# Eight experts of a mixture layer in another order: full and small ones in turn

## The chip, the cores and the metric

The kernel runs on one core of a Trainium2 chip. Its engines are TensorE (PE, matrix products), VectorE (DVE), ScalarE (ACT), GpSimd (POOL) and SyncE (SP, which here only issues the transfers of weights). The metric is the device time of one execution in microseconds (us); lower is better.

## The reference

Two decoder layers work on 256 tokens of width 1024. Each has a mixer (windowed attention beside a diagonal state-space part) and a feed-forward part. In the first layer the feed-forward part is dense; in the second each token goes to 2 of 8 experts, and it is this part that the change touches:

```python
def _swiglu(h, wg, wu, wd):
    return (jax.nn.silu(h @ wg) * (h @ wu)) @ wd

def _moe_swiglu(x2d, w_router, wg, wu, wd):
    logits = (x2d @ w_router).astype(jnp.float32)
    top_v, top_i = lax.top_k(logits, TOP_K)          # TOP_K = 2
    gates = jax.nn.softmax(top_v, axis=-1).astype(x2d.dtype)
    ...
    # every expert: its tokens' rows, SwiGLU with wg[e], wu[e] (1024 x 3584) and wd[e] (3584 x 1024),
    # times the gate, added to those tokens' rows
```

All is float32. The weights of the eight experts are 352 MB and are read once.

## The kernel before

**Tiles of weights.** An expert's inner width 3584 is cut into 7 chunks of 512. A chunk needs 12 tiles of weights of 128x1024 (512 KB each): 4 for the gate, 4 for the up product, 4 for the down product. So an expert has 84 tiles and the part has 672. Each tile is loaded by SP into a buffer `w` (`load`), copied by ACT into a rounded high part `wh`, and DVE subtracts to get the low part `wl` (`split`, line 524). The products are made of three fp32r products, high by high, low by high and high by low (`mm3`), so that they are nearly exact.

**Full and small experts.** After the routing the experts other than number 0 are sorted by how many tokens they got (`sort`). Four of them are full: 128 rows each, three matmuls of 512 columns for each half of a weight tile, 6 per tile (`glu_up`, `glu_down`). Four are small: at most 64 rows each, so that the high and the low part of the rows stand side by side in the 128 columns that PE holds, and 4 matmuls per tile do (`light_up`, `light_down`). The two halves of the result are then joined: ACT copies the lower 64 rows into `low`, and one more matmul adds them to the upper ones (`join`, line 1399), twice per chunk and twice when the expert is done. A tile costs DVE and ACT the same in both kinds. Tokens over these limits are handled by a part behind a branch (`overflow`) that is not entered here.

**Gathering and scattering rows.** `gather` builds a matrix of zeros and ones (`PP`) that picks an expert's tokens, multiplies the rows (`hnh`, `hnl`) with it on PE, and ACT and DVE write the scaled result as `xh` and `xl`. One gather serves expert 0, one expert 1, one experts 2 and 3 together; `gather_light` does the same for the four small ones at once (`PPl`, `lx`, `PTl`). A finished expert is scattered: `yh` by ACT, `yl` by DVE, matmuls by the transposed matrix, and DVE adds to the rows (`X`, `give`, line 1522).

**What sets the order.** The program is first recorded as a list of operations (`Plan.add`) and then ordered by a planner (`Plan.order`, line 234). It runs a clock per engine with a cost for each operation (`Plan.cost`, line 205) and picks on each engine the ready operation with the longest way to the end. Buffers of 128x1024 are 44 (`NM`), shared by `w`, `wh`, `wl`, rows and matrices; a load waits until one is free, and the buffers that it takes over are fixed by that plan. At most 5 `wh` are alive at a time from the fifteenth chunk on (`KR[7]`), 7 before (`LEAN`). Each engine then runs its instructions in that fixed order, held by semaphores alone. A load costs the planner its bytes at 360 GB/s.

**The order of experts.** `moe` (line 1438) goes through `j` from 0 to 7: four full ones, then four small ones. Rows of the next group are gathered near the end of the expert before it (`mark`). All recorded operations carry line 439, so that the names of tiles tell them apart. Below, a *turn* is one expert's 84 tiles.

Of the kernel before, what the change touches and what calls it, by code (L numbers as in the profile page):

```python
# [22 lines left out]
NE = 8  # L23
NCH = DFF // 512

HEAVY = 4
ROOM = 64
GROUPS = {0: (0,), 1: (1,), 2: (2, 3), 4: None}
HEADS = [0, 4, 1, 5, 2, 6, 3, 7]
EPS = 1e-6  # L30
BIG = 1e30
# [31 lines left out]
class Buf:  # L63
    def __init__(self, plan, kind, shape, dtype, name):
        self.kind, self.shape, self.dtype, self.name = kind, shape, dtype, name
        self.real = None
        self.log = []
        self.users = 0
        self.live = False
        self.cols = int(np.prod(shape[1:]))  # L70
# [72 lines left out]


class Plan:
    between = 0.0027

    def __init__(self):
        self.scratch = bacc.Bacc("TRN2", target_bir_lowering=False, num_devices=1)
        self.tensor, self.vector, self.scalar = Engine(self, "PE"), Engine(self, "DVE"), Engine(self, "ACT")  # L150
        self.gpsimd, self.sync = Engine(self, "POOL"), Engine(self, "DMA")
        self.ops = []
        self.after = []
        self.keep = self.floor = 0
        self.tag, self.bonus = None, {}
        self.most = self.turn = self.turns = 0
        self.n = 0
        self.named = {}
# [45 lines left out]
    @staticmethod  # L204
    def cost(eng, method, a, k):
        size = lambda v: int(np.prod(v.shape[1:]))
        if method == "registers":
            return 0.5
        if eng == "DMA":
            return int(np.prod(a[0].shape)) * 4 / 360e3 + 0.01  # L210
        n = max(size(v) for v in a if isinstance(v, View))
        if eng == "PE":
            if method == "transpose":
                return 2 * size(a[2]) / 2400 + 0.001
            if a[1].buf.dtype == F32R:
                return max(size(a[2]), 256) / 2400 + Plan.between
            return 4 * max(size(a[2]), size(a[1])) / 2400 + 0.0054
        if eng == "ACT":
            return 0.05 + n * 0.000876 + (0.06 if any(isinstance(v, View) for v in k.values()) else 0)
        if eng == "POOL":  # L220
            return max(0.35, 0.05 + n * 0.0006)
        if method in ("tensor_scalar", "tensor_copy"):
            fast = all(v.buf.kind != "ps" for v in a if isinstance(v, View))
            ptr = method == "tensor_scalar" and isinstance(a[2], View)
            return 0.066 + n * (0.00055 if fast else 0.00104) + 0.062 * ptr
        ptr = method in ("scalar_tensor_tensor", "tensor_scalar") and any(isinstance(v, View) for v in a[2:3])
        return 0.068 + n * 0.00104 + 0.062 * ptr
# [6 lines left out]
    def order(self, slots):  # L234
# [65 lines left out]
        while done < n:  # L300
# [83 lines left out]
            if e == "PE":  # L384
                if ticks.get(int(t / TICK) - 1, 0) < WARM:
                    cost *= 2
                m = int((t + cost) / TICK)
                ticks[m] = ticks.get(m, 0) + o["cols"]
# [53 lines left out]
class Kernel:  # L442
# [995 lines left out]
    def moe(self, R):  # L1438
        self.mg = gain = R["prm"][:, 90:98]
        self.plan.tag = "rs"  # L1440
        self.rs = rs = self.inv_rms(self.X, D, "fr")
        self.route(rs, gain)
        self.plan.tag = "moe"
        Plan.between = 0.0135
        self.hold = [self.slot.buf.log[-1][0]] if self.HOLD[0] else []
        self.spare = self.HOLD[1]
        mark, rest, hn = None, None, []
        e = self.a["moe"]
        for j in range(NE):
            if j in GROUPS:  # L1450
                first = j
                self.plan.after = [mark] if j else []
                PT, of, rse = self.gather(GROUPS[j], hn) if j < HEAVY else self.gather_light(hn)
                self.plan.after = []
            n = j - first
            acc = [self.bank(), self.bank()]
            for i in range(NCH):
                i == 0 and self.marks.append((f'e{j}', len(self.plan.ops) + 3))
                if i == self.gate_at - 1:
                    mark = len(self.plan.ops) + 1  # L1460
                if i == self.gate_at:
                    if j == 0:
                        hn = self.split_rows([mark])
                    mark = len(self.plan.ops) + 1
                if j:
                    w = [Late(lambda j=j, i=i, q=q: e[bass.ds(self.regs[j], 1), i, q].rearrange("o p n -> (o p) n")) for q in range(12)]
                else:
                    w = [e[0, i, q] for q in range(12)]
                self.ks = self.LEAN[1] if NCH * j + i < self.LEAN[0] else self.KR[7]
                if j < HEAVY:  # L1470
                    ht = self.glu_up(w[:8], lambda t, k: of(n, k), 1, rse[:, n:n + 1])
                    down, scatter, to = self.glu_down, self.scatter, [acc]
                else:
                    ht = self.light_up(w[:8], lambda k: of(n, k), rse[:, n:n + 1])
                    down, scatter, to = self.light_down, self.scatter_light, acc

                if rest:
                    rest[0](*rest[1:])
                rest = (down, i, w[8:], ht, to, scatter(j, n, PT, acc) if i == NCH - 1 else None)
        rest[0](*rest[1:])  # L1480
        return hn
# [12 lines left out]
    def scatter(self, place, j, PT, acc):  # L1494

        y = []

        def half(h):
            if not y:
                y.extend((self.M("yh", F32R), self.M("yl", F32R)))  # L1500
            c = slice(512 * h, 512 * h + 512)
            self.act(y[0][:, c], acc[h], AF.Copy)
            self.tt(y[1][:, c], acc[h], y[0][:, c].bitcast(F32), OP.subtract)
            self.give(place, h, [[(PT[:, t, j], y[i][:, c]) for i in range(2)] for t in range(2)])

        return half
# [15 lines left out]
    def give(self, place, h, ops):  # L1522
        c = slice(512 * h, 512 * h + 512)
        for t in range(2):
            bank = self.bank()
            for i in range(2):
                self.nc.tensor.matmul(bank, *ops[t][i], start=i == 0, stop=i == 1)
            x = self.X[t][:, c]
            self.stt(x, bank, self.sgt[:, 8 * t + place:8 * t + place + 1], x, OP.mult, OP.add)
            if place == NE - 1:  # L1530
                self.nc.sync.dma_start(self.a["out"][t][:, c], x)

    def overflow(self, hn):
# [199 lines left out]
```

## Time and profile before

| | |
|---|---|
| median of 3 runs | 1472.16 us (1465.4 to 1474.07) |
| profiled execution | 1471.39 us |
| its span, first to last instruction | 1469.5 us |
| PE, DVE, ACT busy | 95%, 84%, 71% of the span |
| TensorE clock granted, mean | 0.988 |
| read from memory | 420 MB |

The page gives busy time of each engine over the whole span. The part with the eight experts fills the stretch from about 490 to 1465 us; the mixers and the dense part come before it. PE's busy time is drawn from modelled ends of pipelined matmuls: PE shows busy while matmuls follow each other, and its share says little of stretches in which it waits between them.

### The profile page before, as it was taken

To read this page: it belongs to the slowest core of one execution; us is meant where nothing else is said; L and a number is where in the kernel's file an instruction comes from. 1 tells how busy PE (TensorE), PEld (TensorE's weight loads), DVE (VectorE), ACT (ScalarE), POOL (GpSimd) and SP (SyncE) were. 2 spreads that over 40 slices of the span, in tenths; PEclk is the share of its full clock that TensorE was granted. 3 is DMA by queue.
4 is the path that set the end of the run, shared out by engine and by line. 5 is a ranking of instruction groups with operands and counts; after the bars stand their busy time and mean duration, and the time that the engine had idled before them with its cause. 6 is when DMAs were issued, how large, how long until landed. Compare 5 with 4: busy or idle time off the path is not lost. (4 is left out here: it accounts for less than half of the span.)

```text
span 1469.5 us, 20817 instructions
## 1 busy us (share of the span) xinstructions
PE 1400.5 (95%) x6558; PEld 1065.1 (72%) x6558; DVE 1239.3 (84%) x1668; ACT 1047.4 (71%) x1350; POOL 25.5 (2%) x44
## 2 busy tenths in 40 slices
PE   7999999999999999999999999998988899899897
PEld 4888888888888888888888888885666565555553
DVE  7888984454785899888889999989998999998987
ACT  5586754444455578777678777878787888888885
POOL 3000100000000000000000000000000000000000
PEclk9999999999999899999999999999999999999998
DMA  5356255555358499899899999989999999999993
GB/s 213 111 175 219 72 177 184 189 183 169 106 196 295 156 341 333 298 355 372 321 370 357 350 377 349 363 320 374 356 365 353 338 378 378 380 382 356 370 385 135
DMA packets 116901, 422.59 MB, mean 288 GB/s; under 512 B 13360, under 2 KB 13872, under 8 KB 116784
## 3 DMA queue, kind: packets, MB, share of 16 engines
q1 hardware_dynamic: 116784, 421.20, 77.8%
q8 instruction: 53, 0.87, 0.2%
q14 instruction: 64, 0.52, 0.1%
HBM read 420.10 MB, written 1.05 MB: 287 GB/s over the span
## 5 line engine op out<-in xcount | busy, mean ns | idle before, releaser
L439 DVE TENSOR_TENSOR wl<-w,wh 128x1024 fp32r<-128x1024 f32 x786 | 918.6, 1217 | 101.3 <-ACT wh L439 65.8
L439 ACT ACTIVATE wh<-w 128x1024 fp32r<-128x1024 f32 x786 | 783.7, 1052 | 113.2 <-PE bank L439 54.4
L439 PE MATMUL bank<-wl,lx 128*128 128x512 f32 x448 | 190.5, 428 | 22.2 <-DVE wl L439 21.9
L439 PE MATMUL bank<-wh,lx 128*128 128x512 f32 x448 | 176.2, 402 | 12.5 <-ACT sg L439 9.2
L439 PE MATMUL bank<-wh,xh 128*128 128x512 f32 x448 | 173.7, 393 | 1.1 <-ACT wh L439 0.6
L439 PE MATMUL bank<-wh,xl 128*128 128x512 f32 x448 | 171.9, 392 | 0.0
L439 PE MATMUL bank<-wl,xh 128*128 128x512 f32 x448 | 170.2, 393 | 0.8 <-DVE wl L439 0.8
L439 PEld LDWEIGHTS bank<-wl,lx 128*128 128x128 f32 x448 | 85.2, 190 | 84.3 <-DVE wl L439 65.7
L439 PE MATMUL bank<-wh,hth 128*128 128x512 f32 x336 | 114.2, 397 | 0.0
L439 PE MATMUL bank<-wl,hth 128*128 128x512 f32 x336 | 113.2, 396 | 0.0
L439 PE MATMUL bank<-wh,htl 128*128 128x512 f32 x336 | 112.8, 396 | 0.0
L439 PEld LDWEIGHTS bank<-wh,lx 128*128 128x128 f32 x448 | 85.5, 191 | 29.3 <-ACT sg L439 12.9
L439 PE MATMUL bank<-wl,ht 128*128 128x512 f32 x224 | 93.1, 434 | 9.6 <-DVE wl L439 9.3
L439 PEld LDWEIGHTS bank<-wl,xh 128*128 128x128 f32 x448 | 84.1, 188 | 20.8 <-DVE wl L439 3.5
L439 PEld LDWEIGHTS bank<-wh,xh 128*128 128x128 f32 x448 | 83.7, 188 | 18.4 <-ACT wh L439 1.4
L439 PEld LDWEIGHTS bank<-wh,xl 128*128 128x128 f32 x448 | 83.7, 188 | 17.7 <-DVE xl L439 0.3
L439 PE MATMUL bank<-wh,hh 128*128 128x512 f32 (+1 forms) x288 | 91.5, 385 | 0.4
L439 PE MATMUL bank<-wl,hh 128*128 128x512 f32 (+1 forms) x288 | 90.1, 381 | 0.0
L439 PE MATMUL bank<-wh,hl 128*128 128x512 f32 (+1 forms) x288 | 89.9, 380 | 0.0
L439 PE MATMUL bank<-wh,ht 128*128 128x512 f32 x224 | 85.8, 414 | 0.6 <-ACT wh L439 0.3
L439 ACT ACTIVATE low<-bank 64x512 fp32r<-64x512 f32 x64 | 37.9, 594 | 56.2 <-PE bank L439 55.8
L439 PEld LDWEIGHTS bank<-wh,htl 128*128 128x128 f32 x336 | 62.6, 188 | 13.0 <-DVE wl L439 0.2
(306 smaller groups left out, 1695.6 us busy)
## 6 DMA issues: line engine op xcount, KB each, us to landing
w<-in_moe_dram SPq DMA_DIRECT2D x672, 512.0 KB, 5.7
w<-in_dense_dram SPq DMA_DIRECT2D x84, 512.0 KB, 4.2
w<-in_wo_dram SPq DMA_DIRECT2D x16, 512.0 KB, 4.0
w<-in_win_u_dram SPq DMA_DIRECT2D x8, 512.0 KB, 5.7
w<-in_win_q_dram SPq DMA_DIRECT2D x8, 512.0 KB, 7.8
w<-in_win_kv_dram SPq DMA_DIRECT2D x4, 512.0 KB, 3.6
w<-in_wglu_dram SPq DMA_DIRECT2D x4, 512.0 KB, 3.6
X<-in_x_dram SPq DMA_DIRECT2D x2, 512.0 KB, 4.1
```

The costliest lines, as they stand in the source:

```text
L439: getattr(engines[o["eng"]], o["method"])(*map(real, o["a"]), **{n: real(v) for n, v in o["k"].items()})
```

## The change

The experts are taken in the order 0, 4, 1, 5, 2, 6, 3, 7: a full one, a small one, and so on. The rows of all four small experts are therefore gathered near the end of the first turn; those of expert 1 in the second turn, those of 2 and 3 in the fourth. Their results are kept by expert (`rows`). The planner's cost of a load falls too: 390 GB/s in place of 360 in the part with the experts. The last expert is number 7, as before.

```diff
-GROUPS = {0: (0,), 1: (1,), 2: (2, 3), 4: None}
+LIGHT = tuple(range(HEAVY, NE))
+
+TURNS = (0, 4, 1, 5, 2, 6, 3, 7)
+GROUPS = {0: (0,), 1: (1,), 2: (2, 3), 4: LIGHT}
...
-            return int(np.prod(a[0].shape)) * 4 / 360e3 + 0.01
+            return int(np.prod(a[0].shape)) * 4 / Plan.rate + 0.01
...
-        Plan.between = 0.0135
+        Plan.between, Plan.rate = 0.0135, 390e3
...
-        for j in range(NE):
+        rows = {}
+        for turn, j in enumerate(TURNS):
             if j in GROUPS:
-                first = j
                 self.plan.after = [mark] if j else []
-                PT, of, rse = self.gather(GROUPS[j], hn) if j < HEAVY else self.gather_light(hn)
+                got = self.gather(GROUPS[j], hn) if j < HEAVY else self.gather_light(hn)
                 self.plan.after = []
-            n = j - first
+                for n, i in enumerate(GROUPS[j]):
+                    rows[i] = (n, *got)
+            n, PT, of, rse = rows[j]
...
-                self.ks = self.LEAN[1] if NCH * j + i < self.LEAN[0] else self.KR[7]
+                self.ks = self.LEAN[1] if NCH * turn + i < self.LEAN[0] else self.KR[7]
...
-            if place == NE - 1:
+            if place == TURNS[-1]:
```

What comes before the experts keeps its order on every engine. In it, three places moved that matter below. First, DVE before, near the end of the second full expert, where the rows of experts 2 and 3 are gathered (`PP` is the picking matrix, `xl` the low part of the rows):

```order
L439 TENSOR_TENSOR wl<-w,wh 128x1024
L439 TENSOR_SCALAR PP<-K,sslot 128x128 x4
L439 TENSOR_TENSOR wl<-w,wh 128x1024
L439 COPY rse<-bank 128x2
L439 TENSOR_TENSOR wl<-w,wh 128x1024 x2
L439 SCALAR_TENSOR_TENSOR xl<-bank,prm_1063,xh 128x256 x2
L439 TENSOR_TENSOR wl<-w,wh 128x1024 x2
L439 SCALAR_TENSOR_TENSOR xl<-bank,prm_1063,xh 128x256 x2
L439 TENSOR_TENSOR wl<-w,wh 128x1024 x2
L439 SCALAR_TENSOR_TENSOR xl<-bank,prm_1063,xh 128x256 x2
L439 TENSOR_TENSOR wl<-w,wh 128x1024 x2
L439 SCALAR_TENSOR_TENSOR xl<-bank,prm_1063,xh 128x256 x2
```

The same engine now, in the second full expert's turn (the third turn):

```order
L443 TENSOR_TENSOR wl<-w,wh 128x1024 x10
L443 SCALAR_TENSOR_TENSOR sg<-bank,rse,sg 128x512
L443 TENSOR_TENSOR wl<-w,wh 128x1024 x3
L443 TENSOR_TENSOR htl<-bank,hth 128x512
L443 TENSOR_TENSOR wl<-w,wh 128x1024 x9
L443 SCALAR_TENSOR_TENSOR sg<-bank,rse,sg 128x512
```

Only the splits of weights and the expert's own steps are left there. The gather stands in the small expert's turn that follows (the fourth):

```order
L443 SCALAR_TENSOR_TENSOR sg<-bank,rsl,sg 64x512
L443 TENSOR_TENSOR wl<-w,wh 128x1024 x2
L443 TENSOR_SCALAR PP<-K,sslot 128x128 x4
L443 TENSOR_TENSOR wl<-w,wh 128x1024
L443 TENSOR_TENSOR ht_8817<-bank,ht_8817 128x4x64
L443 SCALAR_TENSOR_TENSOR sg<-bank,rsl,sg 64x512
L443 SCALAR_TENSOR_TENSOR xl<-bank,prm_1063,xh 128x256 x2
L443 TENSOR_TENSOR wl<-w,wh 128x1024
L443 SCALAR_TENSOR_TENSOR xl<-bank,prm_1063,xh 128x256 x6
L443 COPY rse<-bank 128x2
L443 TENSOR_TENSOR wl<-w,wh 128x1024 x12
```

So a gather that stood among a full expert's tiles now stands among a small one's; that of the single expert 1 likewise went from the first turn to the second. Last, ACT in a later small expert before, one whole chunk (`low` is a join, `ht` the input of the down product):

```order
L439 ACTIVATE wh<-w 128x1024 x3
L439 ACTIVATE low<-bank 64x512
L439 ACTIVATE wh<-w 128x1024 x2
L439 ACTIVATE ht_11743<-bank 128x4x64
L439 ACTIVATE wh<-w 128x1024 x6
L439 ACTIVATE low<-bank 64x512
L439 ACTIVATE wh<-w 128x1024
L439 ACTIVATE sg<-bank,rsl 64x512
```

and now, in the second small expert's turn:

```order
L443 ACTIVATE wh<-w 128x1024 x7
L443 ACTIVATE low<-bank 64x512
L443 ACTIVATE wh<-w 128x1024 x5
L443 ACTIVATE low<-bank 64x512
L443 ACTIVATE sg<-bank,rsl 64x512
L443 ACTIVATE ht_8540<-bank 128x4x64
L443 ACTIVATE wh<-w 128x1024 x4
L443 ACTIVATE ht_8602<-bank 128x4x64
L443 ACTIVATE wh<-w 128x1024 x3
L443 ACTIVATE low<-bank 64x512
L443 ACTIVATE wh<-w 128x1024 x3
L443 ACTIVATE low<-bank 64x512
L443 ACTIVATE wh<-w 128x1024 x8
```

The steady pattern that the third and fourth small turn had before, where a `low` comes two splits after the last tile that it needs, is gone: now 3 to 12 splits lie between, and the distance changes from chunk to chunk, as it did before in the first two small turns (2 to 7 there).

## Rows read from the trace of the kernel before

**Rows 1.** The page: span and busy time of each engine, its share, instructions.

```profile
span 1469.5 us, 20817 instructions
...
PE 1400.5 (95%) x6558; PEld 1065.1 (72%) x6558; DVE 1239.3 (84%) x1668; ACT 1047.4 (71%) x1350; POOL 25.5 (2%) x44
```

**Rows 2.** Windows, one per turn from the second: length, busy time (instructions), clock, DMA share, rate.

```profile
core 0: us, PE busy (x) PEld busy (x) DVE busy (x) ACT busy (x) POOL busy (x), PEclk, DMA share, GB/s
614.00:738.50 124.50, 124.50 (x584) 103.36 (x584) 111.31 (x113) 94.48 (x108) 0.00 (x0) 1.00 0.96 355
738.50:857.10 118.60, 118.60 (x536) 96.90 (x535) 108.02 (x104) 93.58 (x102) 0.00 (x0) 1.00 0.97 360
857.10:981.50 124.40, 124.40 (x587) 102.80 (x586) 112.80 (x119) 95.22 (x109) 0.00 (x0) 1.00 0.93 345
981.50:1096.00 114.50, 101.43 (x413) 72.47 (x411) 110.50 (x112) 96.69 (x115) 0.00 (x0) 0.97 0.96 366
1096.00:1217.30 121.30, 106.31 (x413) 72.80 (x414) 113.14 (x114) 99.01 (x118) 0.00 (x0) 0.96 0.95 361
1217.30:1335.70 118.40, 107.67 (x388) 61.60 (x388) 107.69 (x105) 99.61 (x118) 0.00 (x0) 1.00 0.99 379
1335.70:1455.00 119.30, 108.50 (x392) 62.33 (x392) 108.59 (x105) 99.64 (x117) 0.00 (x0) 1.00 0.88 332
```

**Rows 3.** Windows: the splits on DVE (`wl`) in full and small turns.

```profile
614.00:981.50 367.50, 183.84 (x507) 94.54 (x507) 293.72 (x253) 1.00 0.95 354
981.50:1455.00 473.50, 280.41 (x677) 128.72 (x678) 390.24 (x337) 0.98 0.94 360
```

**Rows 4.** Waits of DVE and ACT, first small turn (981.5 to 1096): total us, times, longest.

```profile
DVE wl L439 <- ACT wh L439: 3.3, 4, 1.8
...
ACT low L439 <- PE bank L439: 11.3, 7, 6.2
```

**Rows 5.** The same of the third small turn (1217.3 to 1335.7).

```profile
DVE wl L439 <- ACT wh L439: 6.8, 12, 0.7
DVE sg L439 <- PE bank L439: 3.2, 6, 0.5
...
ACT low L439 <- PE bank L439: 13.4, 14, 2.1
```

**Rows 6.** Gather of expert 1: duration ns min/median/max, first and last start.

```profile
L439 PE MATMUL bank<-PP,hnh x16: 221/274/275, 590.3 to 593.6; 128*128 128x128 f32 x16
L439 DVE TENSOR_SCALAR PP<-K,sslot x2: 279/280/280, 589.7 to 589.9; 128x128 fp32r<-128x128 f32 x2
...
L439 DVE SCALAR_TENSOR_TENSOR xl<-bank,prm,xh x8: 339/343/353, 594.2 to 596.8; 128x128 fp32r<-128x128 f32 x8
```

**Rows 7.** Gather of experts 2 and 3, DVE.

```profile
L439 DVE TENSOR_SCALAR PP<-K,sslot x4: 280/282/284, 712.0 to 712.6; 128x128 fp32r<-128x128 f32 x4
...
L439 DVE SCALAR_TENSOR_TENSOR xl<-bank,prm,xh x8: 476/478/484, 717.1 to 727.9; 128x256 fp32r<-128x256 f32 x8
```

**Rows 8.** Scatter's low part on DVE: all, and by line in the second pure window (738.5 to 857.1).

```profile
L439 DVE TENSOR_TENSOR yl<-bank,yh x16: 669/676/686, 758.0 to 1460.3; 128x512 fp32r<-128x512 f32 x8, 64x512 fp32r<-64x512 f32 x8
...
L439 DVE TENSOR_TENSOR yl<-bank,yh 128x512 fp32r<-128x512 f32 x4 | 2.7, 685 | 0.0
```

**Rows 9.** Who waited for a load of weights, full turns, then small ones.

```profile
ACT wh L439 <- DMA w<-in_moe_dram: 2.3, 4, 1.2
...
DVE wl L439 <- DMA w<-in_moe_dram: 0.4, 1, 0.4
```

**Rows 10.** The DMA queue's own waits for buffers, full turns, then small ones.

```profile
SPq L439 <- PE bank L439: 203.3, 164, 4.2
...
SPq L439 <- PE bank L439: 233.6, 252, 3.4
```

**Rows 11.** DMA issues: count, KB each, median us from issue to landing.

```profile
w<-in_moe_dram SPq DMA_DIRECT2D x672, 512.0 KB, 5.7
```

**Rows 12.** A window in which the clock fell, early in the second small turn.

```profile
1112.60:1119.40 6.80, 6.17 (x15) 4.82 (x16) 6.80 (x10) 5.53 (x6) 0.00 (x0) 0.50 0.69 264
```

More of the change, by code (lines that the diff above doesn't have):

```diff
@@ L145 @@
 class Plan:
-    between = 0.0027
+    between, rate = 0.0027, 360e3
     def __init__(self):
+        Plan.between, Plan.rate = 0.0027, 360e3
         self.scratch = bacc.Bacc("TRN2", target_bir_lowering=False, num_devices=1)
@@ L1468, in moe @@
                     w = [e[0, i, q] for q in range(12)]
-                self.ks = self.LEAN[1] if NCH * j + i < self.LEAN[0] else self.KR[7]
+                self.ks = self.LEAN[1] if NCH * turn + i < self.LEAN[0] else self.KR[7]
                 if j < HEAVY:
-                    ht = self.glu_up(w[:8], lambda t, k: of(n, k), 1, rse[:, n:n + 1])
+                    ht = self.glu_up(w[:8], lambda t, k, n=n, of=of: of(n, k), 1, rse[:, n:n + 1])
                     down, scatter, to = self.glu_down, self.scatter, [acc]
                 else:
-                    ht = self.light_up(w[:8], lambda k: of(n, k), rse[:, n:n + 1])
+                    ht = self.light_up(w[:8], lambda k, n=n, of=of: of(n, k), rse[:, n:n + 1])
                     down, scatter, to = self.light_down, self.scatter_light, acc
```

## The prediction

> **What bounds the kernel now.** I began with the page's busy shares [rows 1]: PE 95%, DVE 84%, ACT 71%, so no engine is full over the whole span and the question is which one is full where. The windows, one per turn of 84 tiles, answer it [rows 2] (the first turn, left out, is treated below). The count of splits shows that the cuts are right: 253 and 337 for three and four turns, against 252 and 336 [rows 3]. In the full turns PE is busy in every microsecond (118.60 of 118.60) while DVE has 10.6 us to spare. A full turn is thus a matter of PE's work alone. In the small turns the reader is to see the opposite: PE has gaps, and DVE is busy for 110.50 of 114.50, then 113.14 of 121.30, 107.69 of 118.40 and 108.59 of 119.30 us. So a small turn is DVE's work plus what DVE idles: 4.0, 8.2, 10.7 and 10.7 us. The waits say where the idling comes from [rows 4, 5]. ACT, which runs in a fixed order, sits at `low` until PE has finished a bank (11.3 and 13.4 us); the `wh` queued behind it come late, and DVE waits for those (3.3 and 6.8 us). The weights themselves are not late: 2.3 us were waited for loads in the full turns and 0.4 in the small ones [rows 9], while the DMA queue waited over 200 us in either half for a buffer to come free [rows 10]. Yet it isn't far from its end: busy 0.93 to 0.99 of the time except in the last turn, which runs out of loads [rows 2].
>
> **Which time the sum is made against.** The profiled execution took 1471.39 us, 1.9 more than its span and 0.8 below the median of 1472.16.
>
> **Full turns: gathers leave them.** The third turn, with no gather, took 118.60 us; the second, with that of experts 2 and 3, took 124.50, and the fourth, with that of the small ones, 124.40 [rows 2]. A gather on PE's path costs 5.9 and 5.8 us. After the change the order leaves the second to fourth full expert with their own work: minus 11.7. The first turn gets the small experts' gather for that of expert 1. The latter's matmuls take 3.3 us from first to last start [rows 6], which is interleaved, so about 3.6; the other I price at its 5.8 of a full turn: plus 2.2, between nothing (both are 32 matmuls) and 5.8. Sum: **minus 9.5**.
>
> **Small turns: DVE gets more to do.** Added to DVE's 439.9 us in the four windows: for expert 1, 2 x 0.280 + 8 x 0.343 = 3.3 us [rows 6]; for experts 2 and 3, 4 x 0.282 + 8 x 0.478 = 5.0 [rows 7]; and 4 `yl` at 0.68 that stood in a full turn [rows 8] and stand in a small one now, 2.7. ACT's share of these (xh, yh) lies beside, since ACT has 18 to 22 us free per small turn [rows 2]. PE's share costs nothing there as long as PE has gaps. That makes 450.9 us of work. The scatters of the full experts were in small turns already, and those of the small experts stay in them.
>
> **Small turns: what DVE idles.** This can't be read from the trace, since the order of ACT and DVE is new. Bounds: 4.0 us per turn, as the first small turn had, which is the only one that follows a full turn, as all will; and 10.7, as the third and fourth had. Its `low` is early by no fixed distance, as in the first two turns of before. I take 6.0, the middle of the first two (4.0 and 8.2), so 24 us in all. Four small turns then take 474.9 us instead of the present 473.5: **plus 1.4**. With 4.0 it would be minus 6.6, with 10.7 plus 20.2.
>
> **The cheaper load in the planner** costs no instruction. It changes the order, which is in the term above, and how early buffers are handed to loads. **Held tiles:** 44 buffers carry the rows too. Before, a full turn held 8 at most (4 of all rows, 4 of experts 2 and 3) and a small one 9; now both kinds stand together and up to 13 are held. Some 4 loads less are ahead, of 512 KB [rows 11]. At 118.6 / 84 = 1.4 us per tile that is 6 us of cover. I cost it at nothing, because nobody waits for loads now [rows 9]; if the cover goes, that is the third rival.
>
> **Sum:** 1471.4 - 9.5 + 1.4 = **1463 us**, 0.6% below the median. Its own range is 1455 (idle 4.0) to 1472 (idle 8.2).
>
> **What a page says of such a change.** The Trainium skill, Perfetto Trace Analysis, Optimization Strategy, says that a kernel whose most contended engine changes over time may gain by interleaving those regimes. The rows show the two regimes, PE full in one half and DVE in the other. By that rule alone a pair of turns would approach the larger of DVE's and PE's work. DVE's is 108 + 112.7 = 221 us per pair where I have 118.6 + 118.7 = 237, which would be 4 x 16 = 64 us less. The trace does not bear that out at this grain: at most 5 `wh` tiles are split ahead, and 5 tiles are 7 us of a turn of 118. Only the seams can overlap. I give it 0.02.
>
> **Rival 1, faster: seams and idling both gain.** At each of the three new seams from full to small, DVE may run 5 tiles ahead of PE at 98 / 84 = 1.16 us (390.24 / 337 [rows 3]) instead of 1.41: 3 x 5 x 0.25 = 4 us. And if more splits ahead of `low` free DVE to idle 2 us per turn, 16 us go. That gives 1463 - 20 = **1443**. For it speaks the first small turn, where a full turn's lead was used up; against it that even there `low` waited 11.3 us [rows 4]. Chance 0.27.
>
> **Rival 2: no better order.** The small turns idle as the third and fourth do, 10.7 us each: 1463 + 18.8 = **1482**, within 1%. For it: the second small turn had an irregular order too and lost 8.2, with a lower clock (0.96) [rows 2]; a piece of it ran at 0.50, the lower of the two levels, 1.2 GHz [rows 12]. Against: it is the worst of four. Chance 0.12.
>
> **Rival 3, slower: the stream of weights becomes the bound.** My sum asks for 84 tiles, 44.0 MB, in 118.7 us, which is 371 GB/s in every turn. The full turns saw 345 to 360 [rows 2]. If buffers come free later because 13 are held, and the rate stays at 360, each of seven turns takes 122.3 us: 856 instead of 355.8 + 474.9 = 830.7, so **1489**. It decides as soon as the lead is used up, and `wh` would then wait for loads. For it: the DMA share is 0.93 to 0.99. Against: 379 GB/s were reached in the third small turn, and the lower rates stand where the queue waited for buffers [rows 10]. Chance 0.13.
>
> The Trainium skill, DMA: Bandwidth & Descriptors, Where 436 GB/s comes from, sets the memory side at about 358 GB/s per core; by that figure a turn would be 123.0 us, an estimate, and the sum 1494. The 379 of the third small turn [rows 2] are above it, so here the measurement decides against it as a ceiling.
>
> **Chances and range.** A run of this kernel tells about 1% from no change, so the marks are 1457.4 and 1486.9. Forecast 0.45, of which 0.08 lies below 1457; rivals 0.27, 0.12, 0.13; full interleaving 0.02; 0.01 for what I have not thought of. Faster: 0.27 + 0.08 + 0.02 = 0.37; same: 0.37 + 0.12 = 0.49; slower: 0.13 + 0.01 = 0.14. From 1440 to 1486 the range leaves out some 0.08 below and 0.12 above.
>
> **What would show it.** In the profile after: the third, fifth and seventh turn at 117 to 119 us with PE busy throughout; if they stay near 124, the first term is wrong. Small turns of 114 to 122 us with DVE busy 110 to 116 and idle 4 to 8; the fourth turn longest, since the larger gather is in it. Waits of `wh` for loads still in single microseconds; tens would mean rival 3. A clock of 0.50 in stretches that begin full turns, where PE is the bound, would cost half their length and would break the sum.

## The result and the profile after

The changed kernel takes **1454.3 us** (median of 4 runs, 1451.65 to 1456.36); before, in the same comparison, 1470.71. The ratio is 0.9891, interval 0.9854 to 0.9928: 1.1% faster, just past the mark of 1457.4 that told faster from the same, though the interval (0.7 to 1.5%) takes in that mark of 1%. 1463 was forecast: the time lies 0.7 us below the forecast's own range of 1455 to 1472, and inside the whole range of 1440 to 1486. The profiled execution took 1456.36 us, 15.0 less than the one of before [rows 1].

The page's first lines hardly differ from those of before: less idle time, the same work.

```profile
span 1454.5 us, 20913 instructions
...
PE 1395.2 (96%) x6558; PEld 1085.9 (75%) x6558; DVE 1239.1 (85%) x1668; ACT 1049.5 (72%) x1350; POOL 25.4 (2%) x44
```

The windows, one per turn, tell more. The first line is the first turn; then small and full turns alternate, beginning with a small one (columns as in [rows 2]).

```profile
core 0: us, PE busy (x) PEld busy (x) DVE busy (x) ACT busy (x) POOL busy (x), PEclk, DMA share, GB/s
465.20:615.60 150.40, 147.59 (x703) 118.89 (x702) 131.69 (x220) 104.44 (x125) 0.00 (x0) 0.98 0.72 260
...
615.60:736.90 121.30, 112.00 (x450) 80.08 (x449) 111.28 (x118) 101.42 (x125) 0.00 (x0) 0.93 0.95 361
736.90:853.30 116.40, 116.40 (x528) 96.09 (x527) 106.48 (x100) 89.97 (x99) 0.00 (x0) 1.00 1.00 385
853.30:975.90 122.60, 111.61 (x453) 79.39 (x452) 116.34 (x125) 103.47 (x127) 0.00 (x0) 0.94 0.96 369
975.90:1091.70 115.80, 115.80 (x525) 95.57 (x524) 107.62 (x101) 92.72 (x100) 0.00 (x0) 1.00 0.99 375
1091.70:1206.60 114.90, 104.02 (x408) 74.19 (x407) 110.95 (x110) 100.48 (x117) 0.00 (x0) 0.94 0.99 377
1206.60:1321.90 115.30, 115.30 (x523) 93.84 (x522) 105.52 (x100) 91.40 (x102) 0.00 (x0) 1.00 1.00 386
1321.90:1439.30 117.40, 109.11 (x413) 74.49 (x412) 112.81 (x113) 99.78 (x118) 0.00 (x0) 0.94 0.82 315
```

The reader is to see two things. The full turns take 115 to 116 us with PE busy throughout; of those before only the one without a gather, 118.60, comes near [rows 2]. The small turns take 115 to 123, with DVE busy for all but 10.0, 6.3, 4.0 and 4.6 us.

| term | before | forecast | measured |
|---|---|---|---|
| first turn | 148.7 | +2.2 | +1.7 (150.4) |
| second to fourth full expert | 367.5 | 355.8 | 347.5 |
| small turns | 473.5 | 474.9 | 476.2 |
| of that DVE's work | 439.9 | 450.9 | 451.4 |
| of that DVE's idle time | 33.6 | 24.0 | 24.8 |

The differences, 1.7 - 20.0 + 2.7 = -15.6, make up the span's -15.0; what is missing stands before the first turn and after the last.

The first turn of before, which had no row yet:

```profile
465.30:614.00 148.70, 145.97 (x694) 120.77 (x693) 129.66 (x214) 103.29 (x125) 0.00 (x0) 0.97 0.77 279
```

From 615.6 us on, loads are waited for as little as before [rows 9], and ACT sits at `low` for 17.8 us in four small turns, where one turn took 11.3 or 13.4 [rows 4, 5]. First the wait for loads, then that of `low` (total, times, longest):

```profile
DVE wl L443 <- DMA w<-in_moe_dram: 0.4, 1, 0.4
...
ACT low L443 <- PE bank L443: 17.8, 22, 1.8
```

### The profile page after: what moved, and what is told of

It is laid out like the page before. It is cut to its first block, busy times and chain, and to the rows that moved or that the text cites. A ratio compares the mean times of both kernels' runs of the same rounds, so it can differ in the third digit from the quotient of the medians.

```text
span 1454.5 us, 20913 instructions
## 1 busy us (share of the span) xinstructions
PE 1395.2 (96%) x6558; PEld 1085.9 (75%) x6558; DVE 1239.1 (85%) x1668; ACT 1049.5 (72%) x1350; POOL 25.4 (2%) x44
## 5 line engine op out<-in xcount | busy, mean ns | idle before, releaser
L443 PE MATMUL bank<-wh,lx 128*128 128x512 f32 x448 | 181.6, 413 | 18.6 <-ACT sg L443 15.1
L443 PE MATMUL bank<-wl,lx 128*128 128x512 f32 x448 | 186.3, 418 | 5.6 <-DVE wl L443 5.3
L443 PE MATMUL bank<-wl,hth 128*128 128x512 f32 x336 | 115.8, 397 | 0.0
L443 PE MATMUL bank<-wh,hth 128*128 128x512 f32 x336 | 115.7, 398 | 0.0
L443 PE MATMUL bank<-wl,ht 128*128 128x512 f32 x224 | 84.5, 420 | 1.7 <-DVE wl L443 1.7
L443 PEld LDWEIGHTS bank<-wh,hth 128*128 128x128 f32 x336 | 62.3, 188 | 13.9 <-issue 0.5
```

Of the source, the lines that this page charges most:

```text
L443: getattr(engines[o["eng"]], o["method"])(*map(real, o["a"]), **{n: real(v) for n, v in o["k"].items()})
```

## Experiments

Each was timed against the kernel before. The column "2 to 7" is, in the profiled execution, the stretch from the first `wh` of the second turn to the first of the eighth; "8" goes from there to the end of the last `wh`. They leave out what happens before the experts, which a different order also shifts. Medians come from four comparisons, in which the kernel before took 1468.7 to 1472.3, so that kernels are better compared by their ratios. With the cost only and at 375 GB/s the traced execution was the fastest of its kernel's, 8.3 and 5.1 us below the median.

| kernel | median us | ratio, interval | 2 to 7 | 8 |
|---|---|---|---|---|
| before | | 1 | 721.7 | 118.7 |
| the change | 1454.3 | 0.9891 (0.9854 to 0.9928) | 706.3 | 113.6 |
| cost only | 1474.82 | 1.0033 (1.0019 to 1.0047) | 712.5 | 115.3 |
| turns only | 1473.69 | 1.0029 (1.0014 to 1.0043) | 722.2 | 118.2 |
| gather in a full turn | 1460.16 | 0.9934 (0.9914 to 0.9954) | 709.5 | 115.3 |
| less PE in full turns | 1441.38 | 0.9810 (0.9791 to 0.9828) | 686.2 | 120.4 |
| less DVE in small turns | 1447.28 | 0.9854 (0.9833 to 0.9876) | 698.4 | 113.7 |
| chunks alternate | 1455.23 | 0.9898 (0.9869 to 0.9927) | 706.1 | 112.7 |
| gaps filled | 1456.33 | 0.9917 (0.9898 to 0.9937) | 706.0 | 113.3 |
| cheap from the fifth turn | 1458.50 | 0.9930 (0.9908 to 0.9951) | 707.1 | 122.9 |
| cost only, gaps filled | 1469.15 | 0.9976 (0.9963 to 0.9989) | 716.0 | 114.6 |
| 375 GB/s | 1464.74 | 0.9958 (0.9941 to 0.9975) | 707.7 | 121.6 |
| 420 GB/s | 1461.66 | 0.9922 (0.9897 to 0.9946) | 709.0 | 110.9 |
| 40 buffers | 1473.90 | 0.9999 (0.9984 to 1.0014) | 704.5 | 116.2 |

**Each half of the change alone.** The old order of experts with the cheaper load:

```diff
-        Plan.between = 0.0135
+        Plan.between, Plan.rate = 0.0135, 390e3
```

> The old order of experts, and only the planner's load at 390 GB/s. If the gain came from work that leaves the full turns (theory: a full turn is PE's work), those stay at 124.5, 118.6 and 124.4 us, and only the small turns change, by DVE's idle time: 0 to -8 us in all, 1463 to 1471. If the gain came from the cheaper load (rival), the time is near 1455.

The new order with the old cost:

```diff
-        Plan.between, Plan.rate = 0.0135, 390e3
+        Plan.between, Plan.rate = 0.0135, 360e3
```

> The new order of experts with the planner's load at 360 GB/s. By the theory the full turns stay at 115 to 117 us and the small turns may idle more, up to 10.7 us each: 1455 to 1472. By the rival (the cheaper load did it) the time goes back to about 1470, with the full turns long again.

Neither is faster: 1.0033 and 1.0029, both intervals above 1, and both together 0.9891. The new order at 360 GB/s starts well (its third turn, full, takes 115.7 us), but its fifth and sixth turn are these:

```profile
970.90:1095.50 124.60, 123.18 (x536) 95.66 (x534) 110.83 (x108) 91.21 (x103) 0.00 (x0) 1.00 0.98 359
1095.50:1213.70 118.20, 107.29 (x397) 64.67 (x397) 107.82 (x106) 98.18 (x115) 0.00 (x0) 1.00 0.99 374
```

The seventh and eighth repeat them (124.9, 118.2). In the small one DVE idles 10.4 us, about the 10.7 of the two last turns of before. In the full one PE looks busy, yet it is fed piece by piece, as the waits of its fifth turn show (total, times, longest; PEld is the load of a block of weights into PE):

```profile
PEld bank L443 <- DVE wl L443: 4.9, 10, 0.7
...
SPq L443 <- DVE wl L443: 45.6, 53, 2.6
...
DVE wl L443 <- ACT wh L443: 10.6, 8, 1.9
...
ACT sg L443 <- PE bank L443: 18.0, 7, 3.4
```

The same waits in the changed kernel's fifth turn, where PEld has none:

```profile
SPq L443 <- DVE wl L443: 9.6, 17, 1.2
...
DVE wl L443 <- ACT wh L443: 0.9, 2, 0.5
...
ACT sg L443 <- PE bank L443: 3.1, 3, 1.3
```

With loads costed at 360, ACT stands at `sg` until PE is through, the `wh` behind it are late, and DVE waits for them, PE for DVE, and the queue for the buffers that DVE gives back (though no engine waits for a load in this turn). At 390 these waits are short. Not all of the 8.8 us between the two turns is waiting: 10 matmuls of a small expert's scatter stand in this turn (536 matmuls), and in the fourth turn of the change (525 in its fifth).

The cheaper load in the old order does help its small turns, in the one execution traced (fifth to seventh turn; the first of them doesn't gain):

```profile
986.90:1106.00 119.10, 106.85 (x427) 76.84 (x426) 114.89 (x117) 98.03 (x114) 0.00 (x0) 0.94 1.00 386
1106.00:1217.40 111.40, 97.67 (x393) 68.31 (x392) 108.66 (x108) 99.32 (x118) 0.00 (x0) 0.97 1.00 394
1217.40:1329.90 112.50, 102.38 (x389) 68.91 (x389) 109.17 (x108) 98.25 (x118) 0.00 (x0) 0.95 1.00 390
```

These are 11.2 us less than before in three turns, with the DMA engines busy throughout. But its full turns stay at 126.5, 120.8 and 122.2, and that execution, 1466.55 us at a mean granted clock of 0.979, was the fastest of ten; the others took 1472 to 1478 at 0.968 to 0.972. That is taken up below (gaps filled).

**Where the cheap cost is needed.**

```diff
             n, PT, of, rse = rows[j]
+            Plan.rate = 360e3 if turn < 4 else 390e3
```

> Nothing left out; the new order of turns, with loads costed at 360 GB/s as before the change up to the fourth turn and at 390 from the fifth. The order at 360 throughout reached the start of the fifth turn at 970.9 us (from 468.0: 502.9), the changed kernel at 975.9 (from 465.2: 510.7), but then its fifth and seventh turn took 124.6 and 124.9 against 115.8 and 115.3, with loads waiting for VectorE to give buffers back (45.6 us against 9.6). Theory: the cheap cost matters where the lead of loads is used up (6 tiles ahead in the fifth turn at 360, 10 to 13 at 390): the first half as at 360, the second as at 390: 1454.3 - 7.8 = 1446.5, taken as 1443 to 1452. Rival, once an order has come down to 6 tiles ahead it stays there whatever the cost, since the small and full turns give nothing back: fifth and seventh turn 122 to 125, 1465 to 1475. Rival, what the first half gains the second gives back because the stream of weights is the floor: 1453 to 1456.

The fifth and sixth turn:

```profile
968.10:1083.60 115.50, 115.46 (x517) 93.02 (x516) 106.70 (x102) 91.10 (x104) 0.00 (x0) 1.00 0.99 373
1083.60:1204.00 120.40, 108.79 (x414) 72.86 (x413) 110.44 (x110) 97.78 (x115) 0.00 (x0) 0.96 0.97 374
```

None of the three expectations held. The rival that a low lead keeps the full turns slow is refuted: with 2 to 6 loads landed ahead of a chunk's first `wh` (8 to 16 in the change) the fifth and seventh turn take 115.5 and 115.9 us. Nor does the cost of 360 alone make a full turn slow: the third turn, planned with it and with 6 to 10 loads ahead, takes 115.7. The gain of the first half was there (start of the fifth turn 503.4 us after that of the first, 510.7 in the changed kernel), but the sixth and eighth turn gave it back (120.4 and 122.9, DVE idle 10.0 and 12.5), as the last rival had it, but not because of the stream: from 620 us on loads were waited for only 0.3 us in all.

**Other costs.** 375 GB/s and, in a second kernel, 420:

```diff
-        Plan.between, Plan.rate = 0.0135, 390e3
+        Plan.between, Plan.rate = 0.0135, 375e3
```

> The new order of turns, loads costed at 375 GB/s, half way between 360 (1473.7) and 390 (1454.3). If the cost acts as a threshold (an order planned below what the chip delivers over a turn, 375 to 386 GB/s, runs at its planned pace; one planned above it is held by engines): at 375 a turn is planned at 117.4 us against engines' 115 to 117, so near the second case: 1452 to 1460. Rival, the cost acts in proportion: 1464. Rival, each order is a throw of its own and the cost says little: anywhere in 1450 to 1475, no order among 360, 375, 390, 420.

> The new order of turns, loads costed at 420 GB/s, over what the chip delivered in any turn (394 at the most). If a cost above the delivered rate only lets loads be issued as early as buffers allow: 1450 to 1458, as at 390. Rival, an order that counts on loads which come later than planned has VectorE and TensorE wait for them: waits of DVE wl for DMA (0.4 us now) grow to 5 or more, 1460 to 1475. Rival by proportion (20 us for 30 GB/s): 1434.

At 360, 375, 390, 420: 1473.7, 1464.7, 1454.3, 1461.7 us. Up to 390 the time falls in proportion, so the threshold that was expected at 375 isn't there. Each cost gave one order only, and orders can differ by 1 to 2 us per turn without a priced reason (see the gather below), so that the rival by which each order is a throw of its own is not excluded. At 420 waits for loads come to 4.6 us, as against 0.4, but the loss lies elsewhere: from the second turn on it takes 709.0 + 110.9 = 819.9 us, what the change takes (706.3 + 113.6), while the first turn begins 3.6 us later and lasts 3.7 longer than the change's:

```profile
468.80:622.90 154.10, 151.00 (x708) 120.80 (x708) 131.25 (x218) 104.67 (x125) 0.00 (x0) 0.97 0.74 268
```

**What bounds the full turns.** In the second to fourth full expert 28 matmuls each (low by high) are left out:

```diff
-        mm(out, al, bh, start=False, stop=False)
+        if self.omit > 0 and not first:
+            self.omit -= 1
+        else:
+            mm(out, al, bh, start=False, stop=False)
```

> As the change, but in the third, fifth and seventh turn 4 products of low rows per chunk are left out, 28 matmuls of a turn's 504, so the result is less exact. Theory (PE's work sets a full turn): 28 x 0.227 = 6.4 us less in each, 110 us, in all -19, 1435; DVE with 106 to 108 us would then be full. Rival (the stream of weights already sets them, DMA share 1.00 at 385 GB/s): the turns stay at 115 to 116, 1454.

The three full turns, and the stretch from the second to the seventh turn:

```profile
737.40:848.70 111.30, 111.30 (x504) 91.18 (x504) 106.85 (x102) 91.51 (x103) 0.00 (x0) 1.00 1.01 387
...
965.60:1075.90 110.30, 110.29 (x500) 90.44 (x499) 104.25 (x99) 89.92 (x102) 0.00 (x0) 1.00 0.99 384
...
1193.70:1304.40 110.70, 110.70 (x500) 90.77 (x499) 102.90 (x97) 90.27 (x102) 0.00 (x0) 1.00 1.00 384
...
618.20:1304.40 686.20, 651.00 (x2801) 498.64 (x2800) 653.12 (x649) 571.13 (x665) 0.00 (x0) 0.98 0.99 380
```

They shrink by 5.1, 5.5 and 4.6 us. Their windows count 24, 25 and 23 matmuls less than the change's, so each one that is gone gives back 0.21 us, about the pace of the others (0.22 us): PE sets these turns. The second and fourth turn get shorter too (2.1 and 5.7), but the sixth and eighth longer (2.9 and 6.8), so that 13.3 of 23.0 us stay to the end of the weights. Over six turns the DMA engines are at 0.99 and move 380 GB/s, some 20 us below the change's 706.3. That the stream of weights would be the next bound is not shown by this: no engine waits for a load in these turns, the queue still waits 356 us for buffers that PE holds, and a share of 0.97 also goes with 360 GB/s [rows 2], one of 1.00 with 394.

**A gather back in a full turn.** Rows of experts 2 and 3 in the third turn:

```diff
-GROUPS = {0: (0,), 1: (1,), 2: (2, 3), 4: LIGHT}
+GROUPS = {0: (0,), 1: (1,), 5: (2, 3), 4: LIGHT}
```

> As the change, but the rows of experts 2 and 3 are gathered one turn earlier, among a full expert's tiles. Theory: the third turn grows by 5.9 us to 122, the fourth loses DVE's 5.0 us and goes from 122.6 to about 117.5, the sum moves by +1, 1455. Rival (a gather is hidden wherever it stands, the full turns got short through the seams alone): the third turn stays at 116.4.

The third turn goes from 116.4 to 122.7, near the price of 5.9 that the prediction read from the rows of before, so a gather isn't hidden there; the fourth goes from 122.6 to 114.2. Together that is -2.1. By the medians this kernel is 5.9 us slower than the change, by the two traces 4.9 from the second turn on; that stands in the other five turns, 1 to 2 us in each, where the two differ only in the order that the planner found. So where the gather stands is worth less than the first term supposed: a full turn's gain is a small turn's loss.

**What bounds the small turns.** In three small turns one tile per chunk goes without its subtraction:

```diff
+        if self.omit > 0:
+            self.omit -= 1
+            return hi, hi
```

> In turns 2, 4 and 6 (experts 4 to 6, small) one tile in every chunk has no VectorE subtraction (its rounded part is used twice): 7 x 1.22 = 8.5 us of VectorE less in each of three turns, 25.6 us in all; nothing else is left out. If VectorE sets the small turns (121.3, 122.6 and 114.9 us now, VectorE busy 111.3, 116.3 and 111.0): 1454.3 - 25.6 = 1429, taken as 1426 to 1434. Rival, the stream of weights stands next behind VectorE: at the 386 GB/s of the seventh turn a turn's 44.04 MB take 114.1 us, so the three turns cannot all fall by 8.5; they come to about 114 each, -16.5 us, 1438, taken as 1435 to 1442, with DMA at 0.99 or 1.00 in them. Rival, what holds these turns is TensorE behind its falls of the clock (0.93 and 0.94 there): hardly anything, 1449 to 1457, and VectorE's idle time grows by the 8.5.

The three turns:

```profile
614.90:730.40 115.50, 109.62 (x458) 82.66 (x457) 106.13 (x114) 100.60 (x125) 0.00 (x0) 0.93 0.98 380
...
845.80:963.90 118.10, 108.55 (x446) 77.87 (x445) 107.84 (x116) 102.64 (x127) 0.00 (x0) 0.94 0.96 368
...
1080.80:1194.20 113.40, 103.42 (x393) 72.45 (x392) 101.10 (x99) 99.42 (x118) 0.00 (x0) 0.92 0.95 362
```

Of 8.5 us per turn 5.8, 4.5 and 1.5 arrive, and 5 to 7 in the whole (by the ratios, by the medians); the full turns change by -1.0, 1.1 and 3.8. Work falls; the idle time is 9.4, 10.3 and 12.3 where it was 10.0, 6.3 and 4.0, now behind `wh` (9.4 us in the last of them, 1.5 in the change), while ACT waits there for PE at `ht` and `low` (6.7 and 5.3 us). So "DVE's work plus its idle time" is a sum that can be read, but not a bound from which work can simply be taken: ACT's waits for PE come up just behind.

**Falls of the clock.** In the changed kernel the clock falls to 0.50 eleven times in small turns, for 58 us in all, and never in the second to fourth full expert. In the kernel before there were four, 17 us (one of them [rows 12]). The falls came with the cheaper load rather than with the new order: in the traced executions the mean clock is 0.988 before, 0.991 with the turns only, 0.979 with the cost only, 0.976 with both. Here is one: PE's instruction after a wait of 2.69 us for ACT's `sg`, and the stretch from 967.2 us.

```profile
968.04 0.79 PE L443 MATMUL bank<-wh,xh 128*128 128x512 f32 x1 [2.69 <-ACT sg L443]
```

```profile
967.20:974.00 6.80, 5.96 (x14) 3.52 (x14) 5.60 (x7) 3.98 (x6) 0.00 (x0) 0.50 1.02 402
```

At 0.50, the lower of the two levels (1.2 GHz), a matmul takes twice as long (0.79 us here, 0.39 elsewhere), and the fall began while PE waited. In the fourth turn, which has this one, the falls last 13.6 us, not the 17 of the expectation below. To see what the falls cost, PE got a matmul by a small block of zeros after each up tile of the small experts, first in the new order, then in the old one with the cheap cost:

```diff
+                self.nc.tensor.matmul(bank[0:8], self.zero, w[0][:, 0:512], start=False, stop=False, skip_group_check=True)
```

> Nothing left out; in the four small turns one matmul of 128x512 by a block of zeros is added after the four of each up tile, 56 in a turn, 56 x 0.2133 = 12 us of TensorE's time in each (it has 11.0 idle and about 17 us at half clock, 8.5 lost, in the fourth turn). Theory: TensorE's waits of 1 to 3 us in small turns are followed by falls of the granted clock to .50 (58 us in all in the small turns), and VectorE waits behind a slow TensorE for a part of its 24.9 us there. If that is so, the falls go (mean clock 0.976 to 0.99), and half of the 24.9 us with them: 1442, taken as 1436 to 1449. Rival, the falls cost nothing because TensorE has room there: clock up or not, 1452 to 1457. Rival, 12 us more on TensorE make it the bound of the small turns: 1460 to 1475, PE busy throughout.

> The old order of turns with loads costed at 390 GB/s (that alone: 1474.8 us, 5 over before, though its traced execution took 1466.6 with small turns of 111 to 119 us at 386 to 394 GB/s and a granted clock of 0.94 to 0.97 there), and in small turns the matmul by zeros after each up tile, 56 in a turn. If falls of the clock are what kept the cheap cost from paying in the old order (0.971 in the executions of 1472 to 1478, 0.979 in the one of 1466.6): clock 0.99 and 1462 to 1467. Rival, as in the new order the filled gaps change nothing because VectorE and the stream set these turns: clock up, 1472 to 1478.

In the new order the clock rises (second turn 1.00, mean 0.991) and nothing is won: 1456.33 against 1454.3, and stretches equal within 0.6 us in all.

```profile
615.60:732.00 116.40, 113.55 (x501) 78.65 (x500) 110.11 (x115) 100.42 (x124) 0.00 (x0) 1.00 0.98 371
732.00:849.70 117.70, 117.70 (x531) 96.16 (x530) 107.23 (x102) 93.22 (x102) 0.00 (x0) 1.00 1.00 382
```

The second turn is 4.9 us shorter; the full turns, 117.7, 117.7 and 116.8, are 4.7 longer together. What the clock gives back and what the added matmuls take can't be told apart here, so it isn't shown that the falls cost nothing in this order. In the old order the same matmuls win 5.7 us by the medians (ratio 1.0033 to 0.9976; the intervals don't touch), and executions then lie within 5 us of each other, at 0.985 to 0.990. So the falls may explain about half a per cent there; even without them the cheap cost alone is worth 0.2%. That executions of one and the same order are slower at a lower clock (cost only, above) speaks for the falls doing the harm, but that it isn't the slightly different order which the added matmuls bring is not separated.

**Fewer buffers.**

```diff
-    NM = 44
+    NM = 40
```

> The changed kernel with 40 buffers of 512 KB instead of 44; its loads run 8 to 16 tiles ahead of their splitting. If the small turns stay at 115 to 122 as long as 8 or so are ahead: 1452 to 1458, 5 to 12 ahead. Rival, read from the order with the cheap cost from the fifth turn on (3 to 5 tiles ahead; its sixth and eighth turn 120.4 and 122.9 against 114.9 and 113.6): each tile of lead is worth something in the small turns, where the order takes tiles in bursts, and four less make them 2 to 5 us longer each: 1462 to 1472.

The total says the whole gain is gone. The stretch says otherwise: 704.5 + 116.2 = 820.7 us, against 819.9. The 20 us are lost before the experts, whose first `wh` comes at 485.3 instead of 465.2 us. With 5 to 13 loads ahead instead of 8 to 16, the turns together take what they took, so four loads of the cover that the prediction costed at nothing were worth nothing.

**A finer grain.** Pairs of a small and a full expert, chunk by chunk:

```diff
+PAIRS = ((4, 1), (5, 2), (6, 3))
...
+        for a, b in PAIRS:
+            for i in range(NCH):
+                steps += [(a, i), (b, i)]
```

> Nothing left out. The first expert alone, then the pairs (4,1), (5,2) and (6,3) chunk by chunk instead of turn by turn, then the last alone; loads still costed at 390 GB/s. Pairs take 237.7, 238.4 and 230.2 us now, 706.3 in all. If engines are what a pair waits for and full and small chunks can share them (TensorE about 115 + 95 at full clock, VectorE 106 + 112 = 218 us in a pair), VectorE would be next at 218 plus its idle, but the stream of weights comes before that: 88.08 MB at 386 GB/s are 228.2 us, 684.6 for the three pairs, -21.7: 1433, taken as 1430 to 1440, with DMA at 0.98 or more throughout and TensorE's granted clock near 1.00. Rival, the alternation by experts had taken what there is to take (a full turn's loads run ahead into the small one already): within 4 us of 1454. Rival, the finer order makes a full chunk wait for a small one's rows and banks (two pairs of accumulating banks are held of the eight): slower, 1460 to 1475.

The stretch of the second to the seventh turn in this kernel, then in the change:

```profile
620.00:1326.10 706.10, 669.47 (x2844) 510.89 (x2843) 655.21 (x637) 574.87 (x655) 0.00 (x0) 0.98 0.97 375
```

```profile
615.60:1321.90 706.30, 675.13 (x2880) 519.17 (x2879) 658.19 (x649) 579.45 (x664) 0.00 (x0) 0.97 0.98 375
```

The same to 0.2 us, and the first turn 4.8 longer (the rows of expert 1 are gathered there too). The Trainium skill, Perfetto Trace Analysis, Optimization Strategy, says that interleaving regimes may improve a kernel whose most contended engine changes; this finer grain gives nothing more in this kernel. No version tried beats the change with all its work done.

## Why the prediction was right, and where not

The size of the gain was missed: 15 us in the profiled execution where 8 were forecast. The full turns account for 8.3 us of that; the other terms are within 1.3 each.

**First turn (+2.2): right**, 1.7.

**Full turns (-9.5 with the first): the mis-sized term.** 118.6 us each was taken from the one turn of before without a gather; measured 116.4, 115.8 and 115.3, 8.3 less in all. Of a turn's 84 tiles the first four are the down products of the preceding expert's last chunk, because they are issued one chunk late (`rest`). Before, a full expert preceded; now a small one does, whose tiles take 4 matmuls and not 6. The groups of PE's matmuls in the third turn show it (`hth` belongs to a full expert's down product, `ht` and `lx` to a small one's):

```profile
L443 PE MATMUL bank<-wh,hth 128*128 128x512 f32 x47 | 16.7, 400 | 0.0
L443 PE MATMUL bank<-wl,hth 128*128 128x512 f32 x46 | 16.1, 396 | 0.0
L443 PE MATMUL bank<-wh,htl 128*128 128x512 f32 x46 | 15.4, 390 | 0.0
...
L443 PE MATMUL bank<-wh,ht 128*128 128x512 f32 x11 | 4.0, 390 | 0.0
L443 PE MATMUL bank<-wl,ht 128*128 128x512 f32 x10 | 3.7, 399 | 0.0
```

and in the pure turn of before:

```profile
L439 PE MATMUL bank<-wl,hth 128*128 128x512 f32 x58 | 20.3, 400 | 0.0
L439 PE MATMUL bank<-wh,hth 128*128 128x512 f32 x55 | 20.1, 401 | 0.0
L439 PE MATMUL bank<-wh,htl 128*128 128x512 f32 x56 | 19.0, 394 | 0.0
```

Four tiles with two matmuls less are 8. At 118.6 / 536 = 0.22 us that is 1.8 us per turn, 5.3 of the 8.3. The windows count 528, 525 and 523 matmuls in place of 536, 32 less in all and not 24, which at that price is 7.1 us. The rest comes from where a window cuts through tiles (parts of `lx` and `ht` above), and from four matmuls of scatters and their matrices that stood in the pure turn of before:

```profile
L439 PE MATMUL bank<-yh,PT 128*128 128x512 f32 x1 | 0.5, 481 | 0.0
L439 PE MATMUL bank<-yl,PT 128*128 128x512 f32 x1 | 0.4, 389 | 0.0
L439 PE MATMUL bank<-K,PP 128*128 128x128 f32 x2 | 0.4, 274 | 0.0
```

The last 1.2 us have no row of their own. The matmuls of the four tiles went to small turns, where PE has gaps.

**Small turns (+1.4): right in the sum, the idling in part by luck.** Work 451.4 (450.9 forecast), idle 24.8 (24). No turn idled the 6.0 that was taken for each: they span the bounds of 4.0 and 10.7 almost whole, with 4.0 in the sixth turn and 10.0 in the second. And the sum holds for this one order: at 360 GB/s the same turns idle 6.2, 6.3, 10.4 and 10.4, 33.2 us. The fourth turn, with the larger gather, was the longest, as said.

**The cheaper load: here the reasoning failed, though the sum did not.** It was costed at nothing by itself, and alone it brings nothing (1.0033). But the text treated it as an edit whose effect is contained in a guessed idle time. The runs show that both terms hang on it: at 360 GB/s the new order's last four turns are full ones of 124.6 and 124.9 us and small ones that idle 10.4, which is rival 2's condition in half the small turns, with a loss in the full turns that no rival had. The prediction's reasoning, applied to the order alone, would have given much the same 1463; that kernel took 1473.69. So the forecast of 1463 came as near as it did because the two edits were made together, for a reason that it didn't have: in that it was lucky. Which of the many instructions that stand differently does it was not isolated, and each half alone was seen in one order only.

**Rival 1** (1443) had 2 us of idling per turn; none came below 4.0. **Rival 3** (the stream) did not occur: the full turns ran at 375 to 386 GB/s. With less work on PE 380 GB/s were drawn over 686 us, and still nobody waited for a load. The Trainium skill, DMA: Bandwidth & Descriptors, Where 436 GB/s comes from, has about 358 GB/s per core on the memory side; the measured 380 lies above it, so as a ceiling the measurement decides against it.

## What to carry to other kernels

Where a planner fixes the order beforehand, its cost figures are part of the schedule: test a new order of work together with them, two by two, since each half alone may be worth nothing. Price a stretch by counting its own instructions, also those carried over from the work before it, rather than by the nearest stretch that looks alike. And compare stretches as well as totals: with 40 buffers the total hid that the part under study had not changed.

## What the runs showed of the hardware

The clock's falls came with the cheaper load, in either order: the mean granted clock was 0.988 before, 0.991 with the turns only, 0.979 with the cost only and 0.976 in the change, which spent 58 us of its small turns at 0.50 against 17 before, in stretches where PE had waits of 1 to 3 us. Refilling those gaps brought the clock to 0.991 without making this order faster. Through the full turns of the change, and of the kernel with less work on PE, one core drew 375 to 387 GB/s, and 394 in a small turn with the cost only, with its DMA engines busy for 0.99 to 1.01 of the time. A busy share near 1 does not tell the rate: 0.97 went with 360 GB/s before [rows 2].
